# Encoder block on one Trainium2 core: gate and up projections by seven half-size products in place of eight

## The chip, the cores and the metric

The kernel runs on one core of one Trainium2 chip. The time is that of the device, in microseconds (us), for one execution; three runs of the kernel before gave 771.43, 771.52 and 772.36 us. The core has five engines with queues of their own: TensorE (PE, matrix products; its weight loads are listed apart as PEld), VectorE (DVE), ScalarE (ACT), GpSimd (POOL) and SyncE (SP, which only issues transfers here). Each works its queue in order, and they wait for each other through semaphores.

## The reference

One encoder layer on 512 tokens of width 1024, in float32. Two attention branches are merged by gates and projected by `w_out`; then comes a gated feed-forward part, which is what the change touches:

```python
x = x + rmsnorm(merged @ w_out[l], post_mix_w[l])
h = rmsnorm(x, pre_ffn_w[l])
f = (jax.nn.silu(h @ w_gate[l]) * (h @ w_up[l])) @ w_down[l]
x = x + rmsnorm(f, post_ffn_w[l])
```

`w_gate` and `w_up` are 1024 x 2816, `w_down` is 2816 x 1024.

## The kernel before

All large products are float32 by parts: an operand is split into a high part in the type fp32r and a low part, the remainder, and a product is three matmuls into the same bank: high by high, high by low, low by high (`mm3`, lines 143 to 146).

Weights come through the class `Weights` (line 36) in units of 128 x 1024 numbers (512 KB). `load_to` issues a unit's load on SP into one of five `raw` buffers. `split_high` makes the high part on ACT (line 74). `split_low` makes the low part on DVE (line 85) or, for units that are marked `by_dma`, in another way: ACT writes minus the high part (line 82), and a transfer from POOL's queue adds the raw numbers to it (line 83).

The feed-forward part works on the transpose of h, `h2T`: 8 blocks of 128 channels by 512 tokens, each in both parts. It is filled by `to_hT` for 128 tokens at a time: PE transposes (line 250), ACT makes the high part (253), DVE the low part (254). The loop ahead of it (lines 808 to 826, the projection by `w_out`) makes h for four groups of 128 tokens; for the fourth, h is ready last.

`w_gate` and `w_up` are cut into 22 column blocks of 128. Blocks 0 and 1 are worked in two halves of 256 tokens (lines 856 to 872), since the second half needs the fourth token group, whose transposes stand late in the first half. Blocks 2 to 21 take 512 tokens at once (lines 873 to 883): for each block and each of gate and up, 8 channel blocks by 3 matmuls of 512 columns into one bank. `ff_evac` (lines 837 to 844) forms silu(gate) by up: ACT sigmoid (840), two DVE products (841, 842), ACT high part (843), DVE low part (844). The results `fT` are the stationary operand of the projection by `w_down` (lines 899 to 925), which uses all eight banks and ends the kernel. The residual `x2` (four tiles) stays on chip until then.

The order around the change is set by the scheduler of the tile framework for each engine, within the waits that the buffers make. The attention part, ahead of all this, has its own hand-made plan (lines 693 to 725).

Of the kernel before, what the change touches and what calls it, by code (L numbers as in the profile page):

```python
# [24 lines left out]
MID = 18  # L25
WIN = ((0, 192), (64, 248), (192, 248), (320, 192))
# [9 lines left out]
class Weights:  # L36
# [3 lines left out]
    def __init__(self, nc, raw_pool, raw_bufs):  # L40
        self.nc = nc
        self.raw_pool = raw_pool
        self.raw_bufs = raw_bufs
        self.units = []
        self.raws = {}
        self.parts = {}
        self.n_dma = 0
        self.n_split = 0
        self.by_dma = set()

    def add(self, src, shape, place, by_dma=False):
# [58 lines left out]
def block_kernel(ctx: ExitStack, tc: tile.TileContext, x, pre_mix_w, w_in,  # L110
# [38 lines left out]
    class Late:  # L149
# [88 lines left out]
    pmm = ctx.enter_context(tc.tile_pool(name="psA", bufs=2, space=PSUM))  # L238
# [5 lines left out]
    hT = hp.tile([128, KD, 2, S], F32R, tag="hT", name="hT")  # L244
    def to_hT(h, b, dst, pool, tag):
        for g in range(2):
# [4 lines left out]
            hi = dst[:, 4 * g:4 * g + 4, 0, 128 * b:128 * b + 128]  # L251
            lo = dst[:, 4 * g:4 * g + 4, 1, 128 * b:128 * b + 128]
# [36 lines left out]
    def proj_v(nm, b, first=False, mid=None):  # L289
# [9 lines left out]
        for n, (k, pa, pw) in enumerate(ops):  # L299
            if mid and n == MID:  # L300
                mid()
            nc.tensor.matmul(bank, hT[:, k, pa, 128 * b:128 * b + 128],  # L302
# [81 lines left out]
    def feat_slot(unit, evac, start=None):  # L384
        st = {}

        def step(q):
            def go():
# [5 lines left out]
                for k in (2 * q, 2 * q + 1):  # L394
                    mm3(st["bank"], hi[:, k], lo[:, k], hT[:, k, 0], hT[:, k, 1],
# [333 lines left out]
    psB = ctx.enter_context(tc.tile_pool(name="psB", bufs=6, space=PSUM))  # L729
# [11 lines left out]
    for m in range(8):  # L741
# [6 lines left out]
        for k in range(KD):  # L748
            mm3(bank, hi[:, k], lo[:, k], hT[:, k, 0], hT[:, k, 1], k == 0, k == KD - 1)
# [13 lines left out]

    pmw = rp.tile([128, D], F32, tag="raw", name="pmw")
# [9 lines left out]
    h2T = hp.tile([128, KD, 2, S], F32R, tag="hT", name="h2T")  # L774
# [32 lines left out]
    h2 = {}  # L807
    for b in range(NB):
# [17 lines left out]
        h2[b] = post(b, y, ss)  # L826
    W.raw_bufs = 5
# [3 lines left out]
    fT = []  # L831

    def ff_tile():
        p = up2 if len(fT) < 11 else up
        return U(F32R, [128, 2, 512], "f", p)

    def ff_evac(bg_, bu, m, cs):
        n = cs.stop - cs.start
        sg = U(F32, [128, 512], "sg")
        nc.scalar.activation(sg[:, :n], bg_, AF.Sigmoid)  # L840
        nc.vector.tensor_mul(sg[:, :n], sg[:, :n], bg_)  # L841
        nc.vector.tensor_mul(sg[:, :n], sg[:, :n], bu)  # L842
        nc.scalar.activation(fT[m][:, 0, cs], sg[:, :n], AF.Copy)
        nc.vector.tensor_sub(fT[m][:, 1, cs], sg[:, :n], fT[m][:, 0, cs].bitcast(F32))

    def ff_mm(nm, m, cs, bank):
        hi, lo = W.get(UF[nm, m])
        for k in range(KD):
            mm3(bank, hi[:, k], lo[:, k], h2T[:, k, 0, cs], h2T[:, k, 1, cs],
                k == 0, k == KD - 1)  # L850

    bb = {}
    for m in range(2):
        for nm in ("g", "u"):
            bb[nm, m] = psB.tile([128, 512], F32, tag="b", name="b")
    for half in range(2):
        cs = slice(256 * half, 256 * half + 256)
        for m in range(2):
            for nm in ("g", "u"):
# [3 lines left out]
                for k in range(KD):  # L863
                    if last and k == 4:
                        to_hT(h2[3], 3, h2T, psB, "b")
                    mm3(bank, hi[:, k], lo[:, k], h2T[:, k, 0, cs], h2T[:, k, 1, cs],
                        k == 0, k == KD - 1)
            if half == 1:
                fT.append(ff_tile())
                ff_evac(bb["g", m], bb["u", m], m, slice(0, 512))  # L870
                for nm in ("g", "u"):
                    W.drop(UF[nm, m])
    for m in range(2, KF):
        bk = {}
        for nm in ("g", "u"):
            if m == KF - 3:
                W.raw_bufs = 4
            W.split_to(UF[nm, m] + 3)
            bk[nm] = psB.tile([128, 512], F32, tag="b", name="b")
            ff_mm(nm, m, slice(0, 512), bk[nm])  # L880
            W.drop(UF[nm, m])
        fT.append(ff_tile())
        ff_evac(bk["g"], bk["u"], m, slice(0, 512))


    psA_banks = [pmm.tile([128, 512], F32, tag="mm", name="mm") for _ in range(2)]
    banks = psA_banks + [psB.tile([128, 512], F32, tag="b", name="b") for _ in range(6)]
# [10 lines left out]

    def dn_mm(b, n, k):
        hi, lo = W.get(UD[k])  # L900
        ts = slice(128 * b, 128 * b + 128)
        mm3(banks[2 * b + n], fT[k][:, 0, ts], fT[k][:, 1, ts], hi[:, n], lo[:, n],
            k == 0, k == KF - 1)

    for k in range(KO):
        W.split_to(UD[k] + 4)
# [4 lines left out]
    W.split_to(UD[KF - 1] + 1)  # L911
    for b in range(NB):
# [79 lines left out]
```

## Time and profile before

| | us |
|---|---|
| median of three runs (lowest, highest) | 771.52 (771.43, 772.36) |
| the profiled execution, its own time | 772.13 |
| the span of its trace | 770.4 |
| PE busy, by the page | 755.3 (98%) |
| the half-width stage of the feed-forward part | 399.4 to 423.3 |
| its full-width stage | 423.3 to 640.9 |
| the projection by `w_down` and the end | 640.9 to 770.4 |

A matmul's listed length runs from its start to its modelled end and overlaps the next one; what a matmul costs in a row of them is the distance of the starts. The rows of one engine give, for each group, the place, the tiles, the shapes and what the engine waited for ahead of it.

### The profile page before, as it was taken

How to read it: one execution, taken by the hardware profiler on the slowest of the kernel's cores; microseconds unless marked ns; L12 is line 12 of the kernel's file. 1: busy time of each engine (PE TensorE's matmuls, PEld its weight loads, DVE VectorE, ACT ScalarE, POOL GpSimd, SP SyncE). 2: the span in 40 equal slices, each digit the busy share in tenths (PEclk: the TensorE clock that was granted, in tenths of full speed). 3: DMA queues.
4: the chain of work that ended last, by engine and by line, in shares of the span. 5: the costliest groups of instructions: out<-in, count | busy, mean ns of one | idle time of the engine just before them, and what ended most of it. 6: DMA issues, size and time to landing. Idle time of an engine off the chain costs nothing.

```text
span 770.4 us, 9412 instructions
## 1 busy us (share of the span) xinstructions
PE 755.3 (98%) x3640; PEld 630.6 (82%) x3640; DVE 343.8 (45%) x630; ACT 331.4 (43%) x532; POOL 83.3 (11%) x126
## 2 busy tenths in 40 slices
PE   7999999999999999999999999999999999999996
PEld 5887888877888888888889888888888888888884
DVE  5625788888776544564563212112111233122333
ACT  4414655666667532542224544444454532122211
POOL 2001001123320000000001111111111100000000
PEclk9999999999999999999999999999999999999998
DMA  9537645333311223456115999999998972323212
GB/s 244 181 95 205 174 103 153 97 97 95 96 57 55 83 82 91 145 181 172 41 28 127 243 196 199 185 197 194 190 188 199 205 197 83 107 84 97 68 40 70
DMA packets 101564, 102.95 MB, mean 134 GB/s; under 512 B 3424, under 2 KB 85360, under 8 KB 101520
## 3 DMA queue, kind: packets, MB, share of 16 engines
q1 hardware_dynamic: 95648, 81.24, 37.1%
q0 software_dynamic: 5872, 21.11, 15.7%
q8 instruction: 29, 0.48, 0.3%
q14 instruction: 15, 0.12, 0.1%
HBM read 72.98 MB, written 2.10 MB: 97 GB/s over the span
## 4 chain that ended last, share of the span: by engine, by line
PE 88%; DVE 5%; ACT 3%; DMA 2%; issue 1%; SPq 0%; POOL 0%; DVEq 0%; POOLq 0%; ACTq 0%
PE b L144 17%; PE b L146 17%; PE b L145 17%; PE mm L144 8%; PE mm L145 8%; PE mm L146 8%; PE mm L302 5%; DMA raw<-in_w_in_dram 2%; PE s L596 1%; DVE pl L547 1%; ACT p L513 1%; PE t L635 1%; PE tb L250 1%; DVE w L85 1%; PE o L144 1%
## 5 line engine op out<-in xcount | busy, mean ns | idle before, releaser
L74 ACT ACTIVATE w<-raw 128x1024 fp32r<-128x1024 f32 x107 | 112.7, 1055 | 131.4 <-PE b L146 114.4
L144 PE MATMUL b<-h2T,w 128*128 128x512 f32 (+1 forms) x384 | 142.7, 372 | 0.0
L145 PE MATMUL b<-h2T,w 128*128 128x512 f32 (+1 forms) x384 | 142.6, 371 | 0.0
L146 PE MATMUL b<-h2T,w 128*128 128x512 f32 (+1 forms) x384 | 142.6, 371 | 0.0
L85 DVE TENSOR_TENSOR w<-raw,w 128x1024 fp32r<-128x1024 f32 x67 | 82.1, 1226 | 98.2 <-ACT w L74 97.7
L144 PE MATMUL mm<-hT,w 128*128 128x512 f32 x256 | 100.8, 394 | 0.3 <-DVE v L314 0.3
L146 PE MATMUL mm<-hT,w 128*128 128x512 f32 x256 | 99.8, 390 | 0.0
L145 PE MATMUL mm<-hT,w 128*128 128x512 f32 x256 | 99.8, 390 | 0.0
L145 PEld LDWEIGHTS b<-h2T,w 128*128 128x128 f32 x384 | 72.3, 188 | 12.6
L146 PEld LDWEIGHTS b<-h2T,w 128*128 128x128 f32 x384 | 72.3, 188 | 12.6
L144 PEld LDWEIGHTS b<-h2T,w 128*128 128x128 f32 x384 | 72.3, 188 | 12.3
L144 PEld LDWEIGHTS mm<-hT,w 128*128 128x128 f32 x256 | 48.1, 188 | 10.2 <-DVE v L314 0.7
L146 PEld LDWEIGHTS mm<-hT,w 128*128 128x128 f32 x256 | 48.1, 188 | 10.2
L145 PEld LDWEIGHTS mm<-hT,w 128*128 128x128 f32 x256 | 48.1, 188 | 9.3
L83 POOL DMA_DIRECT2D w<-raw x40 | 34.9, 872 | 181.6 <-ACT w L82 168.2
L842 DVE TENSOR_TENSOR sg<-sg,b 128x512 f32<-128x512 f32 x22 | 15.1, 687 | 82.5 <-PE b L146 82.5
L841 DVE TENSOR_TENSOR sg<-sg,b 128x512 f32<-128x512 f32 x22 | 15.1, 687 | 79.5 <-ACT sg L840 79.5
L144 PE MATMUL b<-w,f 128*128 128x512 f32 x108 | 42.5, 394 | 0.0
L146 PE MATMUL b<-w,f 128*128 128x512 f32 x108 | 42.5, 394 | 0.0
L145 PE MATMUL b<-w,f 128*128 128x512 f32 x108 | 42.4, 393 | 0.0
L82 ACT ACTIVATE w<-w 128x1024 fp32r<-128x1024 f32 x40 | 42.1, 1053 | 0.6
L235 POOL TENSOR_TENSOR ss<-ss,mhalf 128x1 f32<-128x1 f32 x16 | 8.7, 546 | 295.6 <-DVE ss L788 260.5
(186 smaller groups left out, 1206.4 us busy)
## 6 DMA issues: line engine op xcount, KB each, us to landing
raw<-in_w_in_dram SPq DMA_DIRECT2D x40, 512.0 KB, 4.1
w<-raw POOLq DMA_DIRECT2D x40, 512.0 KB, 6.1
raw<-in_w_gate_dram SPq DMA_DIRECT2D x22, 512.0 KB, 5.7
raw<-in_w_up_dram SPq DMA_DIRECT2D x22, 512.0 KB, 5.4
raw<-in_w_down_dram SPq DMA_DIRECT2D x22, 512.0 KB, 3.6
K<-K SPq DMA_DIRECT2D x24, 256.0 KB, 3.4
x<-in_x_dram SPq DMA_DIRECT2D x8, 512.0 KB, 9.7
raw<-in_w_out_dram SPq DMA_DIRECT2D x8, 512.0 KB, 4.1
```

What stands on the lines that cost most here:

```text
L74: self.nc.scalar.activation(hi, raw, AF.Copy)
L82: self.nc.scalar.activation(lo, hi.bitcast(F32), AF.Copy, scale=-1.0)
L83: self.nc.gpsimd.dma_start(lo, raw, accum_op=ALU.add)
L85: (engine or self.nc.vector).tensor_sub(lo, raw, hi.bitcast(F32))
L144: nc.tensor.matmul(bank, sh, mh, start=first, stop=False)
L145: nc.tensor.matmul(bank, sh, ml, start=False, stop=False)
L146: nc.tensor.matmul(bank, sl, mh, start=False, stop=last)
L235: nc.gpsimd.tensor_tensor(r, ss, mhalf[:, :1], op=ALU.pow)
L250: nc.tensor.transpose(tb[:, k], h[:, 128 * kk:128 * kk + 128], ident)
L302: nc.tensor.matmul(bank, hT[:, k, pa, 128 * b:128 * b + 128], W.get(UV[nm, k // 2])[pw][:, k % 2], start=n == 0, stop=n == len(ops) - 1)
L841: nc.vector.tensor_mul(sg[:, :n], sg[:, :n], bg_)
L842: nc.vector.tensor_mul(sg[:, :n], sg[:, :n], bu)
```

## The change

The column blocks 2 to 21 of gate and of up are taken by pairs: a pair is 1024 channels by 256 columns. With the channels and the columns halved, a pair of weight blocks is a 2 x 2 matrix of pieces A11, A12, A21, A22 (512 channels by 128 columns each), and h, with channels and tokens halved, one of B11 to B22 (512 channels by 256 tokens). Their product is formed by Strassen's scheme in Winograd's form: seven products of pieces and of sums of pieces instead of eight. S1 to S4 are sums of weight pieces, T1 to T4 sums of pieces of h.

- For each pair and each of gate and up (20 units in all), PE does 7 products of 4 channel blocks by 3 matmuls of 256 columns, 84 in all, in four banks, where it did 48 of 512 columns in two banks.
- Weights, per unit (`pair_steps`): DVE forms S1 to S4 (four operations of 128 x 512); high parts of everything on ACT; the low parts of S1 and S2, and of S3 and S4, on DVE; the low parts of A11 and A12 (512 KB) and of A22 (256 KB) by the transfer from POOL's queue. The steps of unit n+1 are written between the products of unit n.
- h: `to_Q` also keeps the raw transposes (`HR`, two more ACT copies for each 128 tokens). `t_sums` forms T1 to T4 and their parts once, after the fourth token group: four DVE differences, four ACT high parts, four DVE low parts of 128 x 1024.
- The results: per unit two ACT copies and five DVE additions of 128 x 256 out of the banks; then for each pair one sigmoid on ACT and two DVE products of 128 x 1024. The split of the gated product is left to the projection by `w_down` (`f_split`).
- Room: `x2` is written to DRAM from POOL's queue after each token group and is read back on SP near the end. The two bank pools `psA` and `psB` are closed ahead of the projection by `w_out`, and one pool of eight banks is opened.
- Blocks 0 and 1 stay as they were, in halves.

```diff
+    def pair_steps(self, j, stage):
+        nc, place = self.nc, self.pairs[j]
+        st, out = {}, {}
+        def high_low(hi, lo, src, by_dma=False):
+            nc.scalar.activation(hi, src, AF.Copy)
+            if by_dma:
+                nc.scalar.activation(lo, hi.bitcast(F32), AF.Copy, scale=-1.0)
+                nc.gpsimd.dma_start(lo, src, accum_op=ALU.add)
+            else:
+                nc.vector.tensor_sub(lo, src, hi.bitcast(F32))
...
+        def s0():
...
+            hi, lo = place("m0")
+            high_low(hi, lo, r0, True)
+            keep(hi, lo, "A11", "A12")
+        def s1():
+            a11, a12, a21, a22 = st["a"]
+            S = st["S"] = stage()
+            nc.vector.tensor_add(S[:, 512:], a21, a22)
+            nc.vector.tensor_sub(S[:, :512], S[:, 512:], a11)
+        def s2():
+            hi, lo = place("s21")
+            high_low(hi, lo, st["S"])
...
+        def s3():
...
+            nc.vector.tensor_sub(R[:, :512], a11, a21)
+            nc.vector.tensor_sub(R[:, 512:], a12, st["S"][:, :512])
+        def s4():
+            hi, lo = place("s34")
+            high_low(hi, lo, st["R"])
...
+        def s5():
+            hi, lo = place("a22")
+            high_low(hi, lo, st["a"][3], True)
...
+    pstk.close()
+    psB = ctx.enter_context(tc.tile_pool(name="psC", bufs=8, space=PSUM))
...
+            nc.scalar.activation(hi, tb, AF.Copy)
+            nc.vector.tensor_sub(lo, tb, hi.bitcast(F32))
+            nc.scalar.activation(raw, tb, AF.Copy)
...
+        for nm, a, b in (("T1", b12, b11), ("T2", b22, "T1"), ("T3", b22, b12), ("T4", b21, "T2")):
+            t[nm] = U(F32, [128, 4, 256], "Tr")
+            nc.vector.tensor_sub(t[nm], a, t[b] if isinstance(b, str) else b)
+            hi, lo = U(F32R, [128, 4, 256], "Th"), U(F32R, [128, 4, 256], "Tl")
+            nc.scalar.activation(hi, t[nm], AF.Copy)
+            nc.vector.tensor_sub(lo, t[nm], hi.bitcast(F32))
...
+        nc.gpsimd.dma_start(x2d[b], x2[b])
...
+    def ff_out(G, Uu):
+        f = U(F32, [128, 2, 512], "f", up2 if len(F) < 11 else up)
+        nc.scalar.activation(f, G, AF.Sigmoid)
+        nc.vector.tensor_mul(f, f, G)
+        nc.vector.tensor_mul(f, f, Uu)
...
+    ORDER = (("A11", "B11", "A"), ("S2", "T2", "B"), ("S1", "T1", "C"), ("S3", "T3", "D"),
+             ("S4", "B22", "C"), ("A12", "B21", "A"), ("A22", "T4", "D"))
...
+        for i, (sn, tn, c) in enumerate(ORDER):
+            (sh, sl), (th, tl) = parts[sn], TQ[tn]
+            for k in range(4):
...
+                nc.tensor.matmul(bank[c], sh[:, k], th[:, k], start=fst, stop=False, **kw)
+                nc.tensor.matmul(bank[c], sh[:, k], tl[:, k], start=False, stop=False, **kw)
+                nc.tensor.matmul(bank[c], sl[:, k], th[:, k], start=False, stop=lst, **kw)
+            B = bank[c]
+            if i == 0:
+                nc.scalar.activation(pv[:, 0], B, AF.Copy)
+            elif i == 1:
+                nc.vector.tensor_add(pv[:, 1], pv[:, 0], B)
+            elif i == 2:
+                nc.vector.tensor_add(pv[:, 2], pv[:, 1], B)
+            elif i == 3:
+                nc.vector.tensor_add(G[:, 1, 256:], pv[:, 2], B)
+            elif i == 4:
+                nc.vector.tensor_add(G[:, 0, 256:], pv[:, 1], B)
+            elif i == 5:
+                nc.scalar.activation(G[:, 0, :256], B, AF.Copy)
+            else:
+                nc.vector.tensor_add(G[:, 1, :256], pv[:, 1], B)
+            if nxt:
+                nxt.pop(0)()
...
-    for m in range(2, KF):
-        bk = {}
-        for nm in ("g", "u"):
...
-            ff_mm(nm, m, slice(0, 512), bk[nm])
```

Three places of the order, with the names of the changed kernel's lines (its numbers differ from those of the kernel before).

DVE, from the fourth token group into the paired stage. Before, the low parts of h (L254) are followed by the first gated products (L841, L842, L844):

```order
L254 TENSOR_TENSOR h2T_3178<-tb_3616,h2T_3178 128x4x128
L841 TENSOR_TENSOR sg_3684<-sg_3684,b_3521 128x512
L842 TENSOR_TENSOR sg_3684<-sg_3684,b_3522 128x512
L844 TENSOR_TENSOR f_3683<-sg_3684,f_3683 128x512
L841 TENSOR_TENSOR sg_3739<-sg_3739,b_3523 128x512
L842 TENSOR_TENSOR sg_3739<-sg_3739,b_3524 128x512
L844 TENSOR_TENSOR f_3738<-sg_3739,f_3738 128x512
```

Now the same low parts (L867) are followed by T1 to T4 (L878) and their low parts (L881), and then by the first unit's sums of weights (L94, L105, L95):

```order
L867 TENSOR_TENSOR Q_3187<-tb_3644,Q_3187 128x4x128
L878 TENSOR_TENSOR Tr_3652<-HR_3478,HR_3302 128x1024
L881 TENSOR_TENSOR Tl_3655<-Tr_3652,Th_3654 128x1024
L878 TENSOR_TENSOR Tr_3658<-HR_3487,Tr_3652 128x1024
L881 TENSOR_TENSOR Tl_3661<-Tr_3658,Th_3660 128x1024
L878 TENSOR_TENSOR Tr_3664<-HR_3487,HR_3478 128x1024
L881 TENSOR_TENSOR Tl_3667<-Tr_3664,Th_3666 128x1024
L878 TENSOR_TENSOR Tr_3670<-HR_3311,Tr_3658 128x1024
L881 TENSOR_TENSOR Tl_3673<-Tr_3670,Th_3672 128x1024
L94 TENSOR_TENSOR S_3740<-raw_3537 128x512
L105 TENSOR_TENSOR S_3794<-raw_3521,raw_3537 128x512
L95 TENSOR_TENSOR S_3740<-S_3740,raw_3521 128x512
```

All eight operations on T1 to T4 stand ahead of the first unit's S sums in DVE's queue.

DVE, in the middle of the full-width stage. Before, three operations for each block:

```order
L841 TENSOR_TENSOR sg_4234<-sg_4234,b_4177 128x512
L842 TENSOR_TENSOR sg_4234<-sg_4234,b_4208 128x512
L844 TENSOR_TENSOR f_4233<-sg_4234,f_4233 128x512
L841 TENSOR_TENSOR sg_4303<-sg_4303,b_4246 128x512
L842 TENSOR_TENSOR sg_4303<-sg_4303,b_4277 128x512
L844 TENSOR_TENSOR f_4302<-sg_4303,f_4302 128x512
```

Now, for a unit: a gated product (L949 or L950), the sums S2 and S1 (L94, L95) of the next unit, the additions out of the banks (L1023, L1025, L1027, L1029, L1033), the low parts (L75) and the sums S3 and S4 (L105, L106):

```order
L950 TENSOR_TENSOR f_4545<-f_4545,G_4429 128x1024
L94 TENSOR_TENSOR S_4585<-raw_4408 128x512
L95 TENSOR_TENSOR S_4585<-S_4585,raw_4286 128x512
L1023 TENSOR_TENSOR pv_4554<-pv_4554,b_4550 128x256
L1025 TENSOR_TENSOR pv_4554<-pv_4554,b_4551 128x256
L75 TENSOR_TENSOR w_4601<-S_4585,w_4601 128x1024
L1027 TENSOR_TENSOR G_4553<-pv_4554,b_4552 128x256
L105 TENSOR_TENSOR S_4617<-raw_4286,raw_4408 128x512
L106 TENSOR_TENSOR S_4617<-raw_4286,S_4585 128x512
L1029 TENSOR_TENSOR G_4553<-pv_4554,b_4551 128x256
L75 TENSOR_TENSOR Q_3187<-S_4617,Q_3187 128x1024
L1033 TENSOR_TENSOR G_4553<-pv_4554,b_4552 128x256
```

The work of two purposes, the next unit's weights and this unit's results, alternates in one queue.

PE, at the start of blocks 2 to 21. Before, the last matmuls of the gate's block and the first of the up's:

```order
L144 MATMUL b_3763<-h2T_3178,w_3745 128x512
L145 MATMUL b_3763<-h2T_3178,w_3745 128x512
L146 MATMUL b_3763<-h2T_3178,w_3745 128x512
L144 MATMUL b_3794<-h2T_3178,w_3751 128x512
L145 MATMUL b_3794<-h2T_3178,w_3751 128x512
L146 MATMUL b_3794<-h2T_3178,w_3751 128x512
```

Now the end of the first unit's product A11 by B11 (bank b_3817), and then the starts of the next three products (S2 by T2 in b_3818, S1 by T1 in b_3819, S3 by T3 in b_3820):

```order
L1018 MATMUL b_3817<-Q_3186,w_3712 128x256
L1016 MATMUL b_3818<-Th_3660,w_3767 128x256
L1017 MATMUL b_3818<-Tl_3661,w_3767 128x256
L1016 MATMUL b_3819<-Th_3654,w_3767 128x256
L1017 MATMUL b_3819<-Tl_3655,w_3767 128x256
L1016 MATMUL b_3820<-Th_3666,Q_3187 128x256
L1017 MATMUL b_3820<-Tl_3667,Q_3187 128x256
L1018 MATMUL b_3818<-Th_3660,w_3767 128x256
L1016 MATMUL b_3818<-Th_3660,w_3767 128x256
```

In this first unit the products are interleaved: two matmuls of each, then the rest of S2 by T2; in all later units they stand one after the other.

## Rows read from the trace of the kernel before

**Rows 1.** The page, part 1: engine, busy us, share, instructions

```profile
PE 755.3 (98%) x3640; PEld 630.6 (82%) x3640; DVE 343.8 (45%) x630; ACT 331.4 (43%) x532; POOL 83.3 (11%) x126
```

**Rows 2.** The page, part 4: shares of the chain that ended last

```profile
PE 88%; DVE 5%; ACT 3%; DMA 2%; issue 1%; SPq 0%; POOL 0%; DVEq 0%; POOLq 0%; ACTq 0%
```

**Rows 3.** Stages: length, busy us (instructions) by engine, clock, DMA, GB/s

```profile
core 0: us, PE busy (x) PEld busy (x) DVE busy (x) ACT busy (x) POOL busy (x), PEclk, DMA share, GB/s
100.00:150.00 50.00, 49.67 (x288) 43.27 (x287) 42.63 (x117) 30.95 (x79) 5.40 (x23) 1.00 0.46 118
...
424.00:640.00 216.00, 216.00 (x955) 178.84 (x954) 44.37 (x63) 99.15 (x117) 32.53 (x38) 1.00 0.90 196
```

**Rows 4.** PE's timeline, full width, first and last: start, us, line, tiles

```profile
423.25 0.40 PE L144 MATMUL b<-h2T,w 128*128 128x512 f32 x1
...
640.65 0.39 PE L146 MATMUL b<-h2T,w 128*128 128x512 f32 x1
```

**Rows 5.** PE's timeline, second half-width pass: first and last

```profile
411.73 0.28 PE L144 MATMUL b<-h2T,w 128*128 128x256 f32 x1
...
423.13 0.28 PE L146 MATMUL b<-h2T,w 128*128 128x256 f32 x1
```

**Rows 6.** PE's timeline in the projection by w_down, twelve matmuls

```profile
642.27 0.40 PE L144 MATMUL b<-w,f 128*128 128x512 f32 x1
...
644.84 0.39 PE L146 MATMUL b<-w,f 128*128 128x512 f32 x1
```

**Rows 7.** Groups by shape, DVE and ACT: busy us, mean ns, idle before

```profile
L85 DVE TENSOR_TENSOR w<-raw,w 128x1024 fp32r<-128x1024 f32 x67 | 82.1, 1226 | 98.2 <-ACT w L74 97.7
L85 DVE TENSOR_TENSOR wlo<-raw,whi 128x1024 fp32r<-128x1024 f32 x14 | 18.1, 1299 | 3.8 <-ACT whi L74 3.8
L844 DVE TENSOR_TENSOR f<-sg,f 128x512 fp32r<-128x512 f32 x22 | 15.2, 691 | 18.5 <-ACT f L843 18.5
L567 DVE TENSOR_TENSOR yt<-o,yb 64x256 f32<-64x256 f32 x16 | 6.8, 422 | 0.5
L74 ACT ACTIVATE w<-raw 128x1024 fp32r<-128x1024 f32 x107 | 112.7, 1055 | 131.4 <-PE b L146 114.4 <-issue 8.0 <-PE mm L302 7.7
L840 ACT ACTIVATE sg<-b 128x512 f32<-128x512 f32 x22 | 13.2, 598 | 63.2 <-PE b L146 63.2
L566 ACT ACTIVATE yb<-o 64x256 fp32r<-64x256 f32 x16 | 6.0, 377 | 11.5 <-DVE yb L568 9.7 <-PE o L558 1.6
```

**Rows 8.** The step from w_branch_a to w_out: timeline of PE and DVE

```profile
352.20 0.39 PE L146 MATMUL b<-ya,w 128*128 128x512 f32 x1
...
352.43 0.40 PE L144 MATMUL b<-whi,mg 128*128 128x512 f32 x1
...
352.72 0.68 DVE L756 TENSOR_TENSOR sig<-sig,b 128x512 f32<-128x512 f32 x1
```

**Rows 9.** DVE's timeline after the fourth token group's transposes

```profile
410.69 1.29 DVE L254 TENSOR_TENSOR h2T<-tb,h2T 128x512 fp32r<-128x512 f32 x2 [2.69 <-ACT h2T L253]
415.50 0.69 DVE L841 TENSOR_TENSOR sg<-sg,b 128x512 f32<-128x512 f32 x1 [3.52 <-ACT sg L840]
```

**Rows 10.** The accumulating transfer's line (L83): issue to landing

```profile
DMA to landing us min/median/max: 4.7/6.1/8.6
```

**Rows 11.** The weight loads' line (L62), 425 to 640 us: issue to landing

```profile
DMA to landing us min/median/max: 3.6/5.7/7.3
```

**Rows 12.** PE's timeline near the start

```profile
8.95 1.32 PE L250 MATMUL tb<-ident,h 128*128 128x128 f32 x8 [1.95 <-DVE h L283]
```

**Rows 13.** Stages near the start, columns as in rows 3

```profile
10.00:12.00 2.00, 1.78 (x6) 1.04 (x5) 1.89 (x4) 1.89 (x3) 0.00 (x0) 0.65 0.95 203
12.00:14.00 2.00, 2.00 (x6) 1.58 (x5) 1.89 (x2) 0.73 (x1) 0.00 (x0) 0.50 1.03 297
14.00:16.00 2.00, 1.27 (x5) 0.74 (x5) 0.88 (x2) 1.42 (x3) 1.06 (x2) 0.99 1.10 326
```

More of the change, by code (lines that the diff above doesn't have):

```diff
@@ L48, in __init__, with add, add_pair @@
         self.n_split = 0
-        self.by_dma = set()
-    def add(self, src, shape, place, by_dma=False):
+        self.pairs = {}
+    def add(self, src, shape, place):
         self.units.append((src, shape, place))
-        if by_dma:
-            self.by_dma.add(len(self.units) - 1)
         return len(self.units) - 1
+    def add_pair(self, srcs, shape, place):
+        j = len(self.units)
+        self.units += [(src, shape, None) for src in srcs]
+        self.pairs[j] = place
+        return j
@@ L154, in __call__ @@
             return self.fn()
+    class Late1(Late):
+        def __call__(self, what):
+            return self.fn(what)
     start_place = Late()
@@ L301, in proj_v @@
                 mid()
[L302 removed]
+            nc.tensor.matmul(bank, hT[k // 4][:, k % 4, pa, 128 * b:128 * b + 128],
                              W.get(UV[nm, k // 2])[pw][:, k % 2],
@@ L887, in block_kernel @@
-    banks = psA_banks + [psB.tile([128, 512], F32, tag="b", name="b") for _ in range(6)]
+                    first = first or steps_of(0)
+                    first.pop(0)()
+    for fn in first:
+        fn()
+    G, Uu = U(F32, [128, 2, 512], "G"), U(F32, [128, 2, 512], "G")
+    for m in range(2):
+        nc.scalar.activation(G[:, m], bb["g", m], AF.Copy)
+        nc.vector.tensor_copy(Uu[:, m], bb["u", m])
+    ff_out(G, Uu)
+    ORDER = (("A11", "B11", "A"), ("S2", "T2", "B"), ("S1", "T1", "C"), ("S3", "T3", "D"),
+             ("S4", "B22", "C"), ("A12", "B21", "A"), ("A22", "T4", "D"))
@@ new lines, in block_kernel @@
+    gu = {}
+    for n, unit in enumerate(pairs):
+        nxt = steps_of(n + 1)
+        parts = W.parts.pop(unit)
+        bank = {c: psB.tile([128, 512], F32, tag="b", name="b")[:, :256] for c in "ABCD"}
+        G = U(F32, [128, 2, 512], "G")
+        pv = U(F32, [128, 3, 256], "pv")
+        for i, (sn, tn, c) in enumerate(ORDER):
+            (sh, sl), (th, tl) = parts[sn], TQ[tn]
+            for k in range(4):
+                fst, lst = i < 4 and k == 0, k == 3
+                kw = {"skip_group_check": True} if i >= 4 else {}
+                nc.tensor.matmul(bank[c], sh[:, k], th[:, k], start=fst, stop=False, **kw)
[18 more added lines that the diff above has]
+                nxt.pop(0)()
+        gu[n % 2] = G
+        if n % 2:
+            ff_out(gu[0], gu[1])
@@ L888, in block_kernel @@
+    banks = [psB.tile([128, 512], F32, tag="b", name="b") for _ in range(8)]
     pow_ = rp.tile([128, D], F32, tag="raw", name="pow")
@@ L911, in block_kernel @@
     W.split_to(UD[KF - 1] + 1)
+    x2 = []
+    for b in range(NB):
+        f_split()
+        t = U(F32, [128, D], "x2")
+        nc.sync.dma_start(t, x2d[b])
+        x2.append(t)
     for b in range(NB):
```

148 lines of the change are left out of this document (97 added, 51 removed).

## Prediction, made before the changed kernel ran

> **What bounds the kernel now.** I read the page's busy shares first: TensorE is busy for 755.3 of 770.4 us [rows 1]. Then the chain that ended last: 88% of it is TensorE, DVE has 5% and DMA 2% [rows 2]. Then the stages. From 424 to 640 us, where the change works, TensorE is busy for 216.00 of 216.00 us at full clock, and DVE for only 44.37; the DMA engines carry 0.90 of what they can [rows 3]. Nothing holds TensorE up there, so only fewer or shorter matmuls help. A matmul's price is the distance of two starts: 960 matmuls of 512 columns, the first at 423.25, the last at 640.65, give 217.40/959 = 0.2267 us [rows 4]. For 256 columns, 96 matmuls of the second half-width pass give 11.40/95 = 0.120 us [rows 5]. Half the columns cost 53% of the time.
>
> **The products.** A unit (a pair for gate or for up) was 48 matmuls, 48 x 0.2267 = 10.88 us, and is now 84 of 256 columns, 84 x 0.120 = 10.08 us. The gain of 0.80 a unit is 7% rather than an eighth, since the smaller matmul is dearer by the column. Over 20 units: **-16.0** (217.6 to 201.6). The break-even is a distance of 10.88/84 = 0.1295 us.
>
> **The bank pools.** With `psA` and `psB` closed, the first matmul of the `w_out` projection can't start until the last reader of the old pools is done. It started at 352.43; DVE's line 756, which reads a bank, ran from 352.72 to 353.40 [rows 8]. So TensorE waits: **+1.0**.
>
> **The start of the paired stage.** Here the order matters. The low part of the last token group ended at 411.98 [rows 9]; T1 can start about there. Each of T1 to T4 is a difference on DVE, a high part on ACT and a low part on DVE, of 128 x 1024, at 1.23, 1.06 and 1.23 us [rows 7]; all eight DVE operations stand in one row ahead of the first unit's sums, and each low part makes the queue wait for ACT. With a few hundredths per hand-over that is 4 x 3.55, to about 426.2. Then come three sums of 128 x 512 (0.69 each, the row of line 844 [rows 7]), to 428.2, and ACT's high part of S1 and S2, to about 429.3. TensorE is through the first product at 423.25 + 12 x 0.120 = 424.7, and every product that stands next needs a sum: a wait of **4.6**. In this unit PE's order has two matmuls each of S2 x T2 and S1 x T1 and then goes to S3 x T3, whose weights need S4's sum (behind one copy out of a bank on DVE, to 429.6) and ACT's high part, to about 431.0: 1.2 more. Then 0.2 for the low part of S1 and S2 (1.23 on DVE). DVE is now behind with the low part of S3 and S4 (432.6), both gated products of blocks 0 and 1 (1.23 each) and the bank additions among them; the fifth product rewrites a bank that the addition at 436.5 reads, which costs 0.5. The next unit's minus high part comes from ACT at about 434.5; with the median landing of 6.1 us [rows 10] the low parts of A11 and A12 are there at 440.6, and are wanted at 439.6: 1.0 (0 to 3.5 by the landings of 4.7 to 8.6). The sum is **+7.5**. The first unit's own accumulated low part lands at 423.05 by the median and costs nothing; the slowest landing would take its time out of the 4.6.
>
> **The clock.** After an idle stretch of 1.95 us ahead of the matmuls at 8.95 [rows 12] the granted clock was 0.65 in 10 to 12 us, 0.50 (the lower of its two levels, 1.2 of 2.4 GHz) in 12 to 14 and 0.99 in 14 to 16 [rows 13]. The work lost there is 2 x 0.35 + 2 x 0.50 = 1.7 us. An idle stretch of 4.6 us may do the same, here while TensorE waits again anyway. Between 0 and 1.7 I take **+1.0**, nearer to the row, less what the waits of 1.2 and 0.5 hide.
>
> **The later units.** DVE per unit: four sums and half of a gated pair's two products, 4 x 0.69 + 1.23; two low parts, 2 x 1.23; five bank additions, which have no row in before. Their bounds are 0.42 (64 x 256, on chip) and 0.69 (twice the columns); a product with a bank as operand took 0.68 at 512 columns [rows 8] against 0.69 without one [rows 7], so I take 0.42. The sum is 8.5 of the unit's 10.08 us: 85% where it was 21%. At 100 to 150 us DVE was busy for 42.63 of 50 with TensorE at 49.67 [rows 3], the same share, without harm. Followed in its order, the tightest place is the addition that must free the bank of the third product (S1 x T1) before the fifth product starts, 5.76 us into the unit; it ends at 4.9, with 0.8 us to spare. So no wait: **0**. With 0.69 an addition, all five of them add 1.3, the two or three ahead of that place use up the 0.8, and the DVE case below holds. ACT has about 6.7 us a unit: three high parts and one minus high part of 128 x 1024 (4 x 1.06), the two of A22 at 128 x 512 (2 x 0.60), two copies out of banks (2 x 0.38) and half a sigmoid (0.53) [rows 7]. The low part of A22 is wanted last, 19 us after the unit's steps begin, and lands at 14.7, at worst 17.2. Weight loads land in at most 7.3 us [rows 11] and have 5 to 12. What POOL's transfers add falls from 1 MB to 0.75 MB a unit, so the DMA share of 0.90 does not rise.
>
> **The rest.** Writing `x2` out is four transfers issued on POOL, which is 11% busy [rows 1]; reading it back is 2 MB under the projection by `w_down`. The splits moved there are 11 ACT and 11 DVE operations of 1.06 and 1.23 us, beside some 129 us of matmuls. All of it is off TensorE's path: 0. If that cover were gone, the first split alone (2.3 us) would be seen.
>
> **The sum.** -16.0 + 1.0 + 7.5 + 1.0 = -6.5. The profiled execution took 772.13, its span and 1.7 around it; that gives 765.6. It lies 0.6 above the median of the runs, so I predict **765.0**.
>
> **The rivals.** *The start is smooth* (the first sums run earlier, or the waits overlap): 7.5 and 1.0 go, 756.6. For it: those waits come from a few operations that could be elsewhere. Against: the queues are in order, and they stand as they stand. Chance 0.08.
>
> *The half-size matmul is dearer than 0.120 here.* The pass that I read it from is only 11 us long, with one weight load for each matmul, as here. In the `w_down` stage the 512-column distance was 2.57/11 = 0.234 [rows 6], 3% above the full-width stage, from operands alone. The same 3% on 0.120 costs 0.0037 x 1680 = 6.2 us: 771.2, no measurable change. Chance 0.12. The Trainium skill's page "TensorE: Matmul & The Clock Gate", section "Back-to-back issue gap", says that the spacing of matmuls, each with a weight load, is set by both, with 81 ns at 128 columns and 131 at 512; an estimate on a line between these is 98 ns at 256, by which a unit would become 31% longer and the kernel end near 838 us. The trace differs at both sizes it shows (0.2267 at 512, 0.120 at 256), so I leave 0.01 for a distance beyond the break-even of 0.1295.
>
> *DVE becomes the bound.* This one ends slower. DVE's operations last as in the rows of one stage, but the same form takes 1.23 in one row and 1.30 in another [rows 7], and bank additions have no row. With 0.8 us to spare in a unit, operations may be 10% longer; from there each per cent costs 20 x 0.085 = 1.7 us, and by 15% all of the gain is gone: 765.6 + 8.5 = about 774. Sums on DVE, copies on ACT and POOL's adding transfers run beside each other more densely than anywhere before, which speaks for it; the stage at 100 to 150 us speaks against. Chance 0.16.
>
> **How the numbers follow.** The forecast keeps 0.63, from 760.5 (landings early, no clock loss, half of the late waits gone) to 769.9. The range runs from 757 to 774: it leaves out the smooth start, and the upper half of the DVE case. A measurement of this kernel tells 0.2% (1.5 us) from no change. Faster: 0.63 + 0.08 = 0.71. Same: 0.12. Slower: 0.16 + 0.01 = 0.17.
>
> **What would show it.** In the profile of the changed kernel: a gap of 4 to 5 us on PE one product into the paired stage, ended by ACT's high part of S1 and S2; a few gaps of about 1 us in the next 17 us, and none by the third unit; a granted clock below 1 right behind the first gap; 0.120 us between matmuls; 201.6 + 7.5 us for the stage; DVE busy for about 85% of it; a gap of 1 us ahead of `w_out`, ended by DVE. The prediction is wrong if PE waits in every unit (for a bank addition or a low part), if the distance is 0.124 or more, or if the T1 to T4 steps start long after 412.

## The result, and the profile after

The changed kernel takes 761.51 us (median of four runs, 761.11 to 761.96) against 771.87 for the kernel before in the same session: a ratio of 0.9866, 95% interval 0.9849 to 0.9883. The forecast was 765.0 in a range of 757 to 774. The gain is 10.4 us where 6.5 were forecast from the profiled execution. The profiled execution of the changed kernel is the longest of its four runs (761.96).

The page of the changed kernel, parts 1 and 4 (busy us of each engine; shares of the chain that ended last), answers [rows 1] and [rows 2]:

```profile
PE 738.8 (97%) x4360; PEld 650.6 (86%) x4360; DVE 481.5 (63%) x827; ACT 373.8 (49%) x604; POOL 85.1 (11%) x130
...
PE 85%; DVE 6%; ACT 4%; DMA 2%; issue 1%; SPq 0%; POOL 0%; DVEq 0%; POOLq 0%; ACTq 0%
```

Stages of the changed kernel (columns as in [rows 3]), the start of the paired stage and its steady part:

```profile
424.00:434.00 10.00, 4.80 (x33) 4.40 (x33) 8.88 (x12) 6.61 (x10) 0.87 (x1) 0.89 0.32 71
434.00:444.00 10.00, 10.00 (x69) 10.00 (x69) 7.72 (x13) 6.96 (x9) 1.55 (x2) 0.77 0.66 160
444.00:630.00 186.00, 185.98 (x1571) 185.77 (x1571) 149.17 (x225) 118.17 (x158) 31.11 (x37) 1.00 0.81 186
```

The steady part looks as forecast: TensorE without a gap at full clock, VectorE at 149.17 of 186 us, the DMA share down from 0.90 to 0.81. Nearly all of the stage's loss is in the first 20 us, where TensorE stands idle and then runs at a lower clock.

TensorE's timeline of the changed kernel (start, us, line, tiles; in brackets the idle time before and its releaser): the last matmul ahead of `w_out` and its first; the last of the first unit's first product, which began at 425.00; the two waits; the starts of the fourth unit and of the projection by `w_down`:

```profile
353.32 0.39 PE L208 MATMUL b<-ya,w 128*128 128x512 f32 x1
354.61 0.47 PE L206 MATMUL b<-whi,mg 128*128 128x512 f32 x1 [0.91 <-DVE sig L829]
...
426.30 0.28 PE L1018 MATMUL b<-Q,w 128*128 128x256 f32 x1
431.08 0.39 PE L1016 MATMUL b<-Th,w 128*128 128x256 f32 x1 [4.50 <-ACT w L70]
...
432.51 0.58 PE L1016 MATMUL b<-Th,Q 128*128 128x256 f32 x1 [0.69 <-ACT Q L70]
...
463.52 0.28 PE L1016 MATMUL b<-Q,w 128*128 128x256 f32 x1
...
632.50 0.40 PE L206 MATMUL b<-w,fh 128*128 128x512 f32 x1
```

The first two rows answer [rows 8]: the wait for VectorE ahead of `w_out` is there. The next ones answer [rows 4]: from 463.52 to 632.50 lie 17 units, so a unit takes 168.98/17 = 9.94 us and a matmul 9.94/84 = 0.1183. The stage takes 632.50 - 425.00 = 207.5 us (217.6 before): 20 x 9.94 = 198.8, and 8.7 for the start.

VectorE's timeline in the same place answers [rows 9]:

```profile
412.67 1.29 DVE L867 TENSOR_TENSOR Q<-tb,Q 128x512 fp32r<-128x512 f32 x2 [2.49 <-ACT Q L866]
414.03 1.22 DVE L878 TENSOR_TENSOR Tr<-HR 128x1024 f32<-128x1024 f32 x1
...
426.84 1.23 DVE L881 TENSOR_TENSOR Tl<-Tr,Th 128x1024 fp32r<-128x1024 f32 x1 [1.12 <-ACT Th L880]
427.99 0.68 DVE L94 TENSOR_TENSOR S<-raw 128x512 f32<-128x512 f32 x1
...
429.19 0.68 DVE L95 TENSOR_TENSOR S<-S,raw 128x512 f32<-128x512 f32 x1
```

The chain of T1 to T4 is 14.0 us long with a wait of 1.1 us for ACT in each step, and the sums that TensorE wants stand behind it, as worked out (426.2 was forecast for its end, from a start two us earlier).

**Where the 10.4 us went**, by the starts of the same matmuls in both traces: up to `w_out` +2.2 (354.61 against 352.43); from there to the paired stage -0.4; the paired stage -10.1; the projection by `w_down`, first to last matmul, 119.99 against 121.75, -1.8; the end -0.3.

### The profile page after: what moved, and what is told of

Read it like the earlier page. It is cut to its first block, busy times and chain, and to the rows that moved or that the text cites. A ratio compares the mean times of both kernels' runs of the same rounds, so it can differ in the third digit from the quotient of the medians.

```text
span 760.0 us, 11245 instructions
## 1 busy us (share of the span) xinstructions
PE 738.8 (97%) x4360; PEld 650.6 (86%) x4360; DVE 481.5 (63%) x827; ACT 373.8 (49%) x604; POOL 85.1 (11%) x130
## 4 chain that ended last, share of the span: by engine, by line
PE 85%; DVE 6%; ACT 4%; DMA 2%; issue 1%; SPq 0%; POOL 0%; DVEq 0%; POOLq 0%; ACTq 0%
PE b L1016 9%; PE b L1018 9%; PE b L206 9%; PE b L1017 9%; PE b L208 9%; PE b L207 9%; PE mm L206 7%; PE mm L208 7%; PE mm L207 7%; PE mm L375 5%; DMA raw<-in_w_in_dram 2%; PE s L669 1%; DVE pl L620 1%; ACT p L586 1%; PE t L708 1%
## 5 line engine op out<-in xcount | busy, mean ns | idle before, releaser
L140 ACT ACTIVATE w<-raw 128x1024 fp32r<-128x1024 f32 x67 | 70.4, 1053 | 64.3 <-PE b L208 52.6
L1016 PE MATMUL b<-Th,w 128*128 128x256 f32 x240 | 68.8, 287 | 4.5 <-ACT w L70 4.5
L1018 PE MATMUL b<-Th,w 128*128 128x256 f32 x240 | 68.8, 288 | 0.0
L1017 PE MATMUL b<-Tl,w 128*128 128x256 f32 x240 | 68.6, 286 | 0.0
L206 PE MATMUL b<-w,fh 128*128 128x512 f32 x144 | 56.1, 390 | 0.0
L208 PE MATMUL b<-w,fl 128*128 128x512 f32 x144 | 56.1, 390 | 0.0
L207 PE MATMUL b<-w,fh 128*128 128x512 f32 x144 | 56.0, 389 | 0.0
L1016 PEld LDWEIGHTS b<-Th,w 128*128 128x128 f32 x240 | 46.7, 195 | 4.7 <-ACT w L70 4.7
L1018 PEld LDWEIGHTS b<-Th,w 128*128 128x128 f32 x240 | 46.9, 196 | 0.0
L1017 PEld LDWEIGHTS b<-Tl,w 128*128 128x128 f32 x240 | 46.7, 194 | 0.0
L1016 PE MATMUL b<-Q,w 128*128 128x256 f32 x160 | 44.5, 278 | 0.0
L1017 PE MATMUL b<-Q,w 128*128 128x256 f32 x160 | 44.4, 278 | 0.0
L1018 PE MATMUL b<-Q,w 128*128 128x256 f32 x160 | 44.4, 278 | 0.0
L896 ACT ACTIVATE junk<-b 128x512 f32<-128x512 f32 x16 | 9.6, 597 | 62.5 <-PE b L208 57.6
```

The source lines that it names most:

```text
L140: self.nc.scalar.activation(hi, raw, AF.Copy)
L206: nc.tensor.matmul(bank, sh, mh, start=first, stop=False)
L207: nc.tensor.matmul(bank, sh, ml, start=False, stop=False)
L208: nc.tensor.matmul(bank, sl, mh, start=False, stop=last)
L896: nc.scalar.activation(junk, bs, AF.Square, scale=1.0 / 32.0, accum_out=ss[:, n:n + 1])
L1016: nc.tensor.matmul(bank[c], sh[:, k], th[:, k], start=fst, stop=False, **kw)
```

## Experiments

All were made on the changed kernel, but for one on the kernel before.

**The order at the start** (x1). Is it the place of the T operations in VectorE's queue, or VectorE's total work?

```diff
...
-                        t_sums()
+                        t_sums(("T1", "T2"))
...
                     first.pop(0)()
+                    if (m, nm) == (0, "u"):
+                        first.pop(0)()
+                    if (m, nm) == (1, "g"):
+                        t_sums(("T3", "T4"))
```

> Only the order changes: T3 and T4 are formed after the first unit's sums S2, S1, S3, S4 in place of ahead of them. Theory (TensorE's wait of 4.7 us comes from the eight T operations that stand ahead of the S sums in VectorE's queue): in the profile of the changed kernel T3 starts at 421.0, so the sums can start there and S2's high part is ready at about 424, before 426.4 when TensorE wants it; the waits of 4.7 and 0.85 go. VectorE still has the same work, so 2 to 4 us of waits come back later (the addition that frees a bank, or unit 2's A11 and A12); if none of them is long enough to lower the clock, its 2.9 us go too. 761.5 - 5.5 + 3 - 2.9 = 756, between 754.5 and 759. Rival (VectorE's whole work up to the fifth product sets the end, whatever its order): the wait only moves, 760.5 to 762.

Measured: 756.43 us (ratio to before 0.9803, 0.9788 to 0.9817), 5.1 less than the changed kernel. VectorE and TensorE in its trace:

```profile
421.86 0.69 DVE L94 TENSOR_TENSOR S<-raw 128x512 f32<-128x512 f32 x1
...
423.67 1.22 DVE L882 TENSOR_TENSOR Tr<-HR 128x1024 f32<-128x1024 f32 x1
```

```profile
433.57 0.38 PE L1026 MATMUL b<-Q,w 128*128 128x256 f32 x1 [1.53 <-DMA w<-raw]
437.02 0.38 PE L1024 MATMUL b<-Th,w 128*128 128x256 f32 x1 [0.60 <-ACT w L70]
```

The sums now come ahead of T3; the waits of 4.5 and 0.69 are gone, and two shorter ones stand in their place, for the next unit's transfer and sums. The clock stayed at 1.00. The place in the queue was the cause; some of the wait moved on, as expected.

**The order, further** (x9).

```diff
+        return [s0, s1, s2, s3, s4, s5] if not early else [s0, s5a, s1, s2, s3, s6, s4]
...
+            if n == 0 and i == 0:
+                t_sums(("T4",))
+            if n == 0 and i == 4:
+                ff_out(G0, Uu0)
```

(`s5a` splits A22 at once, and the next unit's `s0` is called ahead of the first unit's last step.)

> Order alone again, taken further: T1 and T2 first, then the first unit's sums, then T3; T4 and the gated product of blocks 0 and 1 go behind the first unit's first and fifth product; the split of A22 and the next unit's split of A11 and A12 (with their transfers) are issued earlier. Theory (each wait of the start comes from a few operations standing in the wrong place): waits of at most 2.5 us remain in all, none long enough for the clock: 761.5 - 5.5 - 2.9 + 1.5 = 754.6, between 753 and 757. Rival (VectorE's work sets the end): 760 or more.

Measured: 756.02 us (0.9797, 0.9782 to 0.9811); in the trace the stage takes 201.5 us against 207.5, and TensorE's waits in it are 1.8 and 0.4. In this version the second unit's S3 and S4 are written before the first unit's fifth product has read its own, so that this product is formed with other numbers and the kernel does not compute the reference. Its work is the same in number, so its time still tells of the order.

**Was it the idle time that lowered the clock?** (x2)

```diff
-        bank = {c: psB.tile([128, 512], F32, tag="b", name="b")[:, :256] for c in "ABCD"}
+        whole = {c: psB.tile([128, 512], F32, tag="b", name="b") for c in "ABCD"}
+        bank = {c: t[:, :256] for c, t in whole.items()}
...
+            if n == 0 and i == 0:
+                for _ in range(36):
+                    nc.tensor.matmul(whole["B"][:, 256:], sh[:, 0], th[:, 0], start=True, stop=True)
```

> Adds 36 matmuls of 256 columns (about 4.3 us), whose result nobody reads, after the first unit's first product, where TensorE waits 4.7 us; nothing else changes. Theory (the clock fell to its lower level because TensorE stood idle there, and this cost 2.9 us): the granted clock stays at 1.00 in 424 to 444 us, the matmuls after the wait are 0.118 apart and not 0.21, and 2.9 us are gained, of which up to 1.5 come back as the two late waits that the slow clock hid (the fifth product's bank, unit 2's A11 and A12): 758.6 to 760.1. Rival (the clock falls for another reason, such as the change of load): the clock falls all the same and the time is 761.5 or more.

Measured: 759.77 us (0.9843, 0.9828 to 0.9857), 1.7 less than the changed kernel with 4.3 us of matmuls more. The changed kernel in steps of 2 us, and then the version with the filling:

```profile
430.00:432.00 2.00, 0.74 (x4) 0.53 (x4) 2.00 (x4) 2.00 (x3) 0.00 (x0) 0.94 0.76 131
432.00:434.00 2.00, 1.49 (x7) 1.49 (x8) 2.00 (x3) 2.00 (x4) 0.00 (x0) 0.50 0.82 224
434.00:436.00 2.00, 2.00 (x11) 2.00 (x11) 1.54 (x3) 1.68 (x2) 0.00 (x0) 0.50 1.10 299
436.00:438.00 2.00, 2.00 (x11) 2.00 (x10) 2.00 (x4) 0.00 (x0) 0.85 (x1) 0.50 0.35 67
438.00:440.00 2.00, 2.00 (x16) 2.00 (x16) 1.33 (x4) 1.33 (x2) 0.00 (x0) 0.85 1.03 197
```

```profile
424.00:434.00 10.00, 9.05 (x74) 8.59 (x73) 8.87 (x11) 6.11 (x9) 0.87 (x1) 1.00 0.25 52
434.00:444.00 10.00, 9.66 (x81) 9.46 (x81) 9.97 (x16) 6.91 (x11) 1.71 (x2) 1.00 0.63 147
```

After 4.5 us of idle time the granted clock was 0.50, the lower of its two levels, for 6 us and more; with the gap filled it was 1.00 throughout. So the idle time caused the fall. The 68 matmuls from 432.51 to the second unit at 443.34 took 10.83 us where 68 x 0.1183 are 8.04: the fall costs about 2.8, which with a few hundredths at the first matmuls is the 2.9 of the expectation. The stage is 2.2 us shorter in this trace (205.3): some 0.7 came back as waits that the slow clock had hidden, such as 0.3 for the next unit's transfer.

The 2.9 are the price in one execution. Through the first three units the versions x5, x14 and x6 below run the same program as the changed kernel. Behind the same gap of 4.5 us their first units took 17.6, 16.7 and 17.3 us, where the changed kernel's took 18.3 (425.00 to 443.34). The first matmul of the first and of the second unit in x14:

```profile
425.52 0.28 PE L1019 MATMUL b<-Q,w 128*128 128x256 f32 x1
...
442.23 0.28 PE L1019 MATMUL b<-Q,w 128*128 128x256 f32 x1
```

By these four traces the fall costs from about 1.3 (2.9 less 18.34 - 16.71) to 2.9 us, an estimate that takes the waits as equal. That the clock falls behind the gap is common to all of them; how much it costs is not.

**The switch of the bank pools** (x3).

```diff
...
-    pstk.close()
-    psB = ctx.enter_context(tc.tile_pool(name="psC", bufs=8, space=PSUM))
...
-        bank = {c: psB.tile([128, 512], F32, tag="b", name="b")[:, :256] for c in "ABCD"}
+        bank = {c: psB.tile([128, 512], F32, tag="b", name="b")[:, :256] for c in "AB"}
+        for c in "CD":
+            bank[c] = pmm.tile([128, 512], F32, tag="mm", name="mm")[:, :256]
...
```

> Undoes the switch of bank pools: psA and psB stay open, and the units' banks C and D come from psA. Theory (the first matmul of w_out waits for VectorE's last read of a bank because the pools are closed there): the wait of 0.9 us ahead of w_out goes and the kernel takes 760.6; the waits at the start of the paired stage stay, or one grows by the same 0.9 if it is set by something that does not move with TensorE. Rival (that wait is hidden anyway by the later ones): 761.5.

Measured: 759.07 us (0.9834, 0.9817 to 0.985), 2.4 less than the changed kernel. TensorE around the step from `w_branch_a` to `w_out`:

```profile
354.04 0.39 PE L208 MATMUL b<-ya,w 128*128 128x512 f32 x1
354.26 0.40 PE L206 MATMUL b<-whi,mg 128*128 128x512 f32 x1
```

The wait is gone: against the changed kernel (353.32 and 354.61) the matmuls stand 0.72 us later just ahead of this place and 0.35 earlier just behind it, a gain of 1.07. That is what was expected. The rest of the 2.4 is not shown to come from the switch: the first unit took 17.4 us in place of 18.3, which lies within the 16.7 to 18.3 of the traces with the same start. In this trace the clock fell while TensorE still stood idle, so that less of the lower stretch met matmuls:

```profile
428.00:430.00 2.00, 0.00 (x0) 0.00 (x0) 2.00 (x4) 0.41 (x1) 0.87 (x1) 0.80 0.18 31
```

In the changed kernel it fell only after 430 us (0.94 in 430 to 432). Why the moment differs is open.

**All of it together** (x12): the order with the second unit's S3 and S4 written in time, the first gated product put into the second unit, and no switch.

> The order of x9 with unit 2's S3 and S4 written only after the first unit has read its own, the gated product of blocks 0 and 1 put into the second unit, and the bank pools of x3 (no switch). Theory (the start's waits come from the order, the wait ahead of w_out from the switch, and they add): 761.5 - 6.0 (stage of x9) - 1.1 (switch) = 754.4, between 752.5 and 755.5, and faster than the changed kernel and the one before. Rival (they overlap): 755.5 to 757.

Measured: 753.47 us (0.9777, 0.9761 to 0.9793; the changed kernel in its own comparison has 0.9866). It beats both kernels. Its stages from 424 us on, columns as before:

```profile
424.00:434.00 10.00, 8.98 (x75) 8.77 (x75) 9.72 (x14) 6.47 (x10) 0.85 (x1) 1.00 0.64 157
434.00:444.00 10.00, 10.00 (x87) 10.00 (x86) 9.90 (x17) 8.62 (x12) 1.71 (x2) 1.00 0.71 133
```

The paired stage takes 200.2 us, of which 1.4 are left for the start, and VectorE is full there (9.72 and 9.90 of 10).

**Why is a half-size matmul cheaper than 0.120?** (x4) By the order and sizes of the pools, hT and Q lie at 142 to 174 KB of each partition in the changed kernel; in the kernel before hT and h2T lay at 69 to 101.

```diff
     rp = ctx.enter_context(tc.tile_pool(name="raw", bufs=5))
+    hp = ctx.enter_context(tc.tile_pool(name="hT", bufs=2))
     up = ctx.enter_context(tc.tile_pool(name="u", bufs=UB))
...
-    hp = ctx.enter_context(tc.tile_pool(name="hT", bufs=2))
```

> Same instructions; only the pool of hT and Q is opened ahead of the pool u, so that hT and Q lie where hT and h2T lay in the kernel before (69 to 101 KB of each partition) and u behind them. Theory (the distance of two matmuls depends on where their operands lie): from 276 to 352 us the distance falls back from 0.2297 to 0.2267 (1 us less); in the second half-width pass it rises from 0.118 to 0.120; a unit becomes longer by about 0.1 (36 of its 84 matmuls move B11, B21 or B22): 9.94 to 10.05, 20 x 0.11 = +2.2; the whole 761.5 - 1.0 - 0.6 + 0.4 + 2.2 = 762.5. Rival (the distances come from something else that the change moved, such as the mix of work beside them): all distances stay, 761.5.

Measured: 762.3 us (0.9879, 0.9866 to 0.9893). The second half-width pass (96 matmuls), first and last, in the changed kernel:

```profile
413.70 0.28 PE L206 MATMUL b<-Q,w 128*128 128x256 f32 x1
...
424.89 0.28 PE L208 MATMUL b<-Q,w 128*128 128x256 f32 x1
```

and with hT and Q back in the old place, with the first matmuls of `w_out`, of the fourth unit and of `w_down`:

```profile
352.85 0.47 PE L206 MATMUL b<-whi,mg 128*128 128x512 f32 x1 [0.96 <-DVE sig L829]
...
412.20 0.28 PE L206 MATMUL b<-Q,w 128*128 128x256 f32 x1
...
423.60 0.28 PE L208 MATMUL b<-Q,w 128*128 128x256 f32 x1
...
461.87 0.28 PE L1016 MATMUL b<-Q,w 128*128 128x256 f32 x1
...
633.23 0.40 PE L206 MATMUL b<-w,fh 128*128 128x512 f32 x1
```

The four times (761.3 to 763.29) overlap with those of the changed kernel, so the time alone decides nothing here; the distances do. The pass goes from 11.19/95 = 0.1178 back to 11.40/95 = 0.120, the value of [rows 5], and a unit from 9.94 to 171.36/17 = 10.08 us, exactly the 84 x 0.120 of the prediction. Ahead of `w_out` the same move gives 1.8 us back (352.85 against 354.61), about 1.5 of it behind the first 30 us, where hT is the moving operand. Same instructions, other addresses: the place of the tiles sets these distances. In the half-width pass hT and Q are the only operands of the matmuls that moved. The pool u (T1 to T4, the sums, the results) moved by 32 KB as well, so in a unit the edit does not tell one operand from another, nor from the tiles of the engines that work beside TensorE.

**The same for the projection by `w_down`** (x13), on the kernel before: the gated products of blocks 0 to 10 lay above 174 KB, those of 11 to 21 below; here they are exchanged. (The last four of the weight blocks of `w_down` change pools too; the matmuls shown below have weights that stayed.)

```diff
-        p = up2 if len(fT) < 11 else up
+        p = up if len(fT) < 11 else up2
...
-        return place_w() if dcnt[0] <= 2 else place_pool(up2)()
+        return place_w() if dcnt[0] <= 2 else place_pool(up)()
```

> The kernel before, with the gated products of the first 11 blocks in the pool u and those of the last 11 in u2 (it was the other way), so that the ones above 174 KB of a partition are now blocks 11 to 21. Theory (in the projection by w_down a matmul is 3% dearer where its stationary operand lies up there, and the change took them all out of there): 642 to 697 us go from 0.2333 to 0.2267 between matmuls, and the blocks from 11 on rise to 0.233 or more; the whole time stays within 1 us. Rival (the distance follows the time or the weights' transfers, not the place): 0.2333 stays in 642 to 697.

Measured: 771.12 us (0.9992, 0.9983 to 1.0001), no change. Twelve matmuls early in the projection, eleven late in it, and the late place in the kernel before:

```profile
642.09 0.39 PE L146 MATMUL b<-w,f 128*128 128x512 f32 x1
...
644.58 0.39 PE L145 MATMUL b<-w,f 128*128 128x512 f32 x1
```

```profile
705.01 0.39 PE L144 MATMUL b<-w,f 128*128 128x512 f32 x1
...
707.35 0.39 PE L145 MATMUL b<-w,f 128*128 128x512 f32 x1
```

```profile
704.99 0.39 PE L146 MATMUL b<-w,f 128*128 128x512 f32 x1
...
707.26 0.39 PE L144 MATMUL b<-w,f 128*128 128x512 f32 x1
```

Early, 2.49/11 = 0.2264 where [rows 6] had 0.2336; late, 2.34/10 = 0.234 where the kernel before had 2.27/10 = 0.227. The dear stretch moved with the tiles. The changed kernel's projection has its split products all below 174 KB, and it is 1.8 us shorter.

**How near is VectorE to being the bound?** (x5, x14, x6) One, two or three further operations in each of the last 16 units:

```diff
...
+            st["hi"], st["lo"] = hi, lo
...
+            for _ in range(1 if late else 0):
+                nc.vector.tensor_sub(st["lo"], st["S"], st["hi"].bitcast(F32))
```

> Adds one VectorE operation of 128 x 1024 to each of the last 16 units (the low part of S1 and S2 is formed a second time, with the same result). VectorE is busy for 149.17 of 186 us in 444 to 630, or 7.97 of a unit's 9.94; the operation adds 1.14. Theory (what counts is VectorE's whole time in a unit, 1.97 free, and its queue catches up): 0 to +1, 761.5 to 762.5. Rival of the prediction's working (0.8 us at the tightest place decides): 16 x (1.14 - 0.8) = +5.4, 767.

> Two further VectorE operations of 128 x 1024 in each of the last 16 units, where x5 had one. With one, VectorE was busy for 115.84 of 130 us in 490 to 620, or 8.86 of a unit's 9.94; the second adds at most 1.14: 10.0. Theory (VectorE's whole time in a unit decides, and it is just used up): 0 to +0.3 a unit, 762 to 767, with VectorE busy for 98% and more. Rival (waits at single places decide before VectorE is full): more than +0.5 a unit, 770 or more.

> Three further VectorE operations of 128 x 1024 in each of the last 16 units: 7.97 + 3 x about 1.0 to 1.14 = 11.0 to 11.4 us of VectorE in a unit of 9.94. Theory (VectorE is then the bound and each further operation costs its own time): +1.0 to +1.5 a unit, 778 to 786, slower than before. Rival (the extra operations slip into idle time still): under 770.

Measured: 761.99 us (0.9875, 0.9861 to 0.9888), 762.17 us (0.9875, 0.9859 to 0.9892) and 804.35 us (1.042, 1.0399 to 1.0441). The stretch from 490 to 620 us of the changed kernel and of the three, in this order:

```profile
490.00:620.00 130.00, 130.00 (x1101) 130.00 (x1101) 103.73 (x159) 82.18 (x112) 22.51 (x27) 1.00 0.80 185
```

```profile
490.00:620.00 130.00, 130.00 (x1101) 130.00 (x1100) 115.84 (x172) 82.40 (x113) 22.38 (x26) 1.00 0.81 185
```

```profile
490.00:620.00 130.00, 130.00 (x1092) 129.62 (x1091) 127.76 (x183) 77.94 (x110) 22.32 (x26) 1.00 0.82 185
```

```profile
490.00:620.00 130.00, 111.98 (x861) 108.64 (x860) 111.70 (x152) 64.91 (x89) 17.24 (x20) 0.95 0.65 146
```

With VectorE at 80 and 89% TensorE stays full. At 98% the row still says full, but 1092 matmuls stand in it and not 1101: 9 x 0.118 = 1.1 us of the 130, or 0.08 a unit, which the projection by `w_down` then starts later. The third operation costs 42.2/16 = 2.6 us a unit, more than twice the 1.1 us that it was expected to add, and 18 us beyond the top of what was expected for the whole. VectorE did not stay full as the theory said: it falls to 86%. TensorE's waits in the last version (us in all, times, longest), the first line and the third:

```profile
PE b L1021 <- DMA w<-raw: 18.6, 9, 3.8
...
PE b L1021 <- DVE w L119: 3.5, 3, 1.2
```

and VectorE's largest wait for TensorE:

```profile
DVE pv L1026 <- PE b L1021: 24.6, 7, 5.7
```

Once the queue no longer catches up within a unit, TensorE waits for the next unit's transfer, and VectorE then waits for TensorE's banks; the two idle in turns, and the clock (0.95) falls with it. One thing here is of this edit and not of VectorE's load alone: the added operations (L119) rewrite the low part of S2 and S1, so the products that read it wait for the last of them. How the transfer came to be late was not traced further.

## Why the prediction came out as it did

| term | forecast | measured | from |
|---|---|---|---|
| products | -16.0 | -18.8 | 20 x 9.94 for 217.6 |
| switch of bank pools | +1.0 | +1.1 | x3 |
| waits at the start | +7.5 | +5.8 | 4.7, 0.85, and 0.3 in the third unit |
| clock after the wait | +1.0 | +2.9 | x2; 1.3 to 2.9 by the traces with the same start |
| other stages' matmuls | 0 | -0.7 | +1.5 (hT), -0.4 (half width), -1.8 (`w_down`) |
| start of the kernel, end | 0 | -0.7 | -0.4 and -0.3, of which runs differ by as much |
| sum | -6.5 | -10.4 | |

**Products: right in kind, mis-sized.** The step that failed is the price: 0.120 was read from one pass with the moving operand in one place and taken as a property of the size. The mean is 0.1183, and with the operands in the old place it is 0.120 to the last digit (x4). This is 2.8 of the 3.9 us by which the sum missed. The rival of a dearer matmul named the right mechanism ("from operands alone"), but I gave it only the upward side.

**Switch: right**, with its size and its releaser.

**Start: the chain was right, the tail was not.** The gap of 4.5 us came where it was forecast, ended by ACT's high part of S2 and S1, and the second, by S3 and S4, was 0.69 where 1.2 were forecast. Of the waits of 0.2, 0.5 and 1.0 behind them none was seen in the first two units, and one of 0.3 in the third: TensorE had become slow meanwhile and wanted everything later. x2, with the clock kept up, shows some of them again. They and the clock were two sides of one cost, and I added both. That the sum came out, 8.5 forecast and 8.7 measured, is luck: two errors of about the same size cancel.

**Clock: too small for the execution in the trace.** I bounded it by the 1.7 us of [rows 13]. There the lower level was granted for 3.4 us, worked out from the shares (0.65 and 0.50 in 2 us each); here for 6.8 (0.94, three times 0.50, 0.85). The traces with the same start lie between 1.3 and 2.9, on both sides of the 1.7: a bound from one row was no bound.

**The rivals.** The smooth start did not come by itself (x1 and x12 show what it is worth: up to 8 us with the switch). VectorE did not become the bound: a unit took 7.97 us of it (149.17 of 186) where 8.5 were added up. The point from which it decides was mis-sized: 0.8 us at the tightest place was not the measure, since a late addition in one unit is caught up in the same unit; 1.8 us more of VectorE's time in a unit (127.76 against 103.73 in 130) cost 0.08 (x14), and only beyond 9.94 us does it decide, in x6 with more than the added operation's own length. The estimate of 98 ns from the Trainium skill's page "TensorE: Matmul & The Clock Gate", section "Back-to-back issue gap", is out here too: 113 to 120 ns were measured at 256 columns. The 838 us given with it leave out the waits and the clock of the other sum (9.5 us).

**No effect, as forecast:** the spill of `x2`, its return and the splits moved to `w_down`. TensorE ran through that projection with no wait.

## What to carry over

A matmul's price read from one stage holds for the place of its operands in that stage; where a change moves tiles, read the distance for old and new places, and give the price a range on both sides. Where a scheme needs sums before its first products, walk the queue that forms them: the order of twelve operations was worth 5 us here. A wait behind which TensorE's clock falls costs a second time, here 1.3 to 2.9 us, and part of the later waits goes at the same time, so the two must not simply be added; how much it costs differs between executions, so compare several traces of the same start before a difference there is put down to an edit. Here VectorE beside the bound could be filled to 89% of a unit for nothing and to 98% for 0.08 us a unit; past that the loss was larger than the work that was added. A busy share does not show such small losses: count the matmuls.

## What the runs showed of the hardware that I had not expected

The distance of two matmuls depends on where their tiles lie (x4, x13), and the same few values recur. For 256 columns, in one unit of the changed kernel (A12 by B21, and then A22 by T4, first and last of 12 each):

```profile
629.70 0.28 PE L1016 MATMUL b<-Q,w 128*128 128x256 f32 x1
...
630.95 0.28 PE L1018 MATMUL b<-Q,w 128*128 128x256 f32 x1
631.06 0.28 PE L1016 MATMUL b<-Th,w 128*128 128x256 f32 x1
...
632.38 0.28 PE L1018 MATMUL b<-Th,w 128*128 128x256 f32 x1
```

That is 1.25/11 = 0.1136 and 1.32/11 = 0.120; for 512 columns it was 0.2267 or 0.2336. The same product has the same distances in unit after unit, whichever of the four weight buffers holds its weights. Which property of the addresses decides was not found: the pass at 413.70 with B12 and B22 has 0.1178, A12 by B21 has 0.1136 with neighbouring addresses. If all 1680 half-size matmuls had 0.1136, the stage would be 1680 x 0.0047 = 7.9 us shorter, an estimate from these rows.
